# Spatial mixing spread between projections, and a first norm's vectors spread by other products

## The chip, the cores and the metric

The kernel runs on one core of a Trainium2 chip. The metric is the device time of one execution in microseconds. The kernel before takes 1092.2 us (median of three runs, 1090.23 to 1094.16). The profile comes from one further execution of 1090.98 us, whose traced span is 1089.2 us; some 1.8 us of it lie around the span.

Engines are named as in the profile: PE multiplies matrices, DVE and POOL work on vectors, ACT does activations and copies, SP and ACT issue the DMAs. Each engine works through its own instructions strictly in order and waits for others by semaphores.

## The reference

A layer norm, then two layers. One layer projects the normed stream (512 tokens, 1024 channels) by one wide matrix, mixes tokens in three ways, projects back and norms again:

```
h = layer_norm(x, ln_in_g, ln_in_b)
for l in range(2):                       # hybrid_layer
    na_q, na_k, na_v, na_z, gq_q, gq_k, gq_v, gq_z, sg_u, sg_v, sg_z, gates = split(h @ w_in + b_in)
    y_a = neighbourhood_attention(na_q, na_k, na_v, na_rpb)
    y_b = gqa_attention(rope(rms_norm(gq_q)), rope(rms_norm(gq_k)), gq_v)
    y_c = sg_u * (w_s @ layer_norm(sg_v) + b_s)      # per chunk of 128 tokens and group of 64 channels
    p_x = (y_x * silu(z_x)) @ w_br_x                 # x = a, b, c
    h = layer_norm(alpha * h + (sum of sigmoid(gate_x) * p_x) @ w_out + b_out)
```

The third mixer is the spatial mixing: a layer norm of `sg_v` over its 512 channels, then in each of four chunks of 128 tokens a product with a 128x128 matrix per channel group, then a sum with a bias. All of it is float32.

## The kernel before

Float32 accuracy on PE comes from splitting both factors into a rounded part (h, float32r) and the rest (l): each product is run three times, h by h, l by h and h by l (`mm3`, L195 to L198). Every weight chunk is loaded by SP as `raw_...`, its rounded part `whi_...` is copied by ACT (L143) and its rest `wlo_...` is subtracted by DVE (L144). A projection group such as `zb` (a gate), `nq`, `nk`, `su` or `sz` has 24 products of 128x128 by 128x512 into one bank of PSUM. PSUM banks come from two sets: `acc` with three buffers and `att` with five.

**The start** (`first_layer_start`, emitted and issued in written order). The rows `x` come in tiles of 128 tokens (`xin`). The first norm's scale and shift lie in DRAM as two rows of 1024. They are loaded to one partition (`lnrow`) and spread over all 128 partitions by four float32 products with a column of ones (`lnb`, L347), each recorded as two passes. DVE applies the norm to tile 0 straight from these four PSUM banks (L359 and L361, two operations for each half of 512 channels), ACT later copies them to `lnc_in` for the other tiles. The weights of the first queries come as four chunks `raw_gq_0` to `_3`; ACT rounds each ("high", L337), and the rest ("low", L340) is made on POOL for chunks 0 and 1 and on DVE for chunks 2 and 3. The power -0.5 of each norm's variance is a small POOL operation (`rs`, L226).

**The middle of a layer.** The work is written as a list of steps; Tile turns it into one order for each engine. First come ten projection chunks (`sv`, `nv`, `zb_0`, `zb_1`), with the rotation and transposes of the grouped-query heads between them (`between`). Then follow units of grouped-query attention: scores `gs`, their row maximum `nm` (DVE), the exponential with its sum (ACT, `gp`), reciprocal and scaling (DVE), transposes `gt` (PE) with copies `gpT` (ACT), and products with the values `gy`. Between units stand the steps of the list `fill`. Spatial mixing is in that list: for chunk c of the tokens n_c is the norm's first half (`svT` transposes on PE, BN_STATS and BN_AGGR on DVE, the power on POOL), and m_c is the rest: the normed chunk `vn` by two DVE operations (L233, which subtracts the mean and scales, and L235, which multiplies by `rs` and adds), eight products `mix` on PE (L536) and four sums `m` on DVE (L540).

Of the kernel before, what the change touches and what calls it, by code (L numbers as in the profile page):

```python
# [9 lines left out]
F32 = mybir.dt.float32  # L10
F32R = mybir.dt.float32r
AF = mybir.ActivationFunctionType
ALU = mybir.AluOpType
# [4 lines left out]
P = 128  # L18
D = 1024
KD = D // P  # L20
S = 512
NT = S // P
# [11 lines left out]
NCHUNK = 4  # L34
# [18 lines left out]
def tile_encoder(ctx: ExitStack, tc: tile.TileContext, a, out):  # L53
    nc = tc.nc
    scalar = nc.scalar
# [14 lines left out]
    act = nc.scalar.activation  # L70
    dve = nc.vector
    pool = nc.gpsimd
    pe = nc.tensor
# [12 lines left out]
    pw = cst.tile([P, 10], F32, name="pw")  # L86
    pool.memset(pw, -0.5)

    one = cst.tile([P, 1], F32, name="one")
    pool.memset(one, 1.0)  # L90
    bcol = cst.tile([P, DEPTH, NCOL], F32, name="bcol")
    hcol = cst.tile([P, DEPTH, NCOL], F32, name="hcol")
    bvg = cst.tile([P, DEPTH, NKV], F32, name="bvg")
# [20 lines left out]
    def psum(tag, name):  # L114
        return pp.tile([P, S], F32, tag=tag, name=name, bufs=3 if tag == "acc" else 5)

    def t2(name):
        return tp.tile([P, S], F32, tag="t2", name=name, bufs=4)
# [4 lines left out]
    def asf(r):  # L123
        return r.bitcast(F32)
# [25 lines left out]
    def step(fn, specs=(), frees=None, into=None):  # L150
        steps.append((fn, list(specs), len(specs) if frees is None else frees, into))
# [167 lines left out]
    def first_layer_start():  # L319
        raw = {}  # L320
        input_load(0)
        rows = rp.tile([P, 2, D], F32, tag="r8", name="lnrow")[0:1]
        scalar.dma_start(rows, a["ln_in_rows"])
        scalar.dma_start(ident, a["ident"])
        for n in ("q0", "q1", 1, "q2", "q3", 2, "k0", 3, "k1"):
            if isinstance(n, int):
                input_load(n)
            else:
                raw[n] = load(*(gqw_spec if n[0] == "q" else kvw_spec)(0, int(n[1])))
        w = {}  # L330

        def high(n):
            if n[0] == "q":
                w[n] = gqw_tile(f"gq0_{n[1]}")
            else:
                w[n] = [wp.tile([P, 4, 256], F32R, tag=t, name=f"{t}_gkv0_{n[1]}") for t in ("whi", "wlo")]
            act(w[n][0], raw[n], AF.Copy)  # L337

        def low(n, engine):
            engine.tensor_tensor(w[n][1], raw[n], asf(w[n][0]), op=ALU.subtract)  # L340

        gains = {}
        lnc = st["lnc"] = cst.tile([P, 2, D], F32, tag="cvec", name="lnc_in")
        for h in range(2):
            for j in range(2):
                ps = gains[j, h] = psum("acc" if h + j < 2 else "att", f"lnb_{h}_{j}")
                pe.matmul(ps, lhsT=one[0:1].broadcast_to([1, P]), rhs=rows[:, j, 512 * h:512 * h + 512],  # L347
                          start=True, stop=True)

        def stats(i):  # L350
            st["stats", i] = row_stats(st["xin", i], D, f"in{i}")

        def apply(i):
            xi, (mv, rs) = st["xin", i], st["stats", i]
            xt = []
            for h in range(2):
                cs = slice(512 * h, 512 * h + 512)
                g, b = [gains[j, h] if i == 0 else lnc[:, j, cs] for j in range(2)]
                dve.scalar_tensor_tensor(out=xi[:, cs], in0=xi[:, cs], scalar=mv[:, 0:1], in1=g,  # L359
                                         op0=ALU.subtract, op1=ALU.mult)  # L360
                dve.scalar_tensor_tensor(out=xi[:, cs], in0=xi[:, cs], scalar=rs, in1=b, op0=ALU.mult, op1=ALU.add)  # L361
                ps = psum("att", f"xt_in{i}_{h}")
                for j in range(4):
                    c = 512 * h + P * j
                    pe.transpose(ps[:, P * j:P * j + P], xi[:, c:c + P], ident)
                xt.append(ps)
            for h in range(2):
                split_x(xt[h], i, h)
            if i:
                scalar.dma_start(hbuf[0][i], xi)  # L370

        stats(0)
        high("q0")
        low("q0", pool)
        high("q1")
        low("q1", pool)
        apply(0)
        high("q2")
        low("q2", dve)
        stats(1)  # L380
        high("q3")
        low("q3", dve)
        for kc in range(4):
            st["gqw", kc] = w[f"q{kc}"]
        gq_queries(0, 0)
        for h in range(2):
            for j in range(2):
                act(lnc[:, j, 512 * h:512 * h + 512], gains[j, h], AF.Copy)
        scalar.dma_start(hbuf[0][0], st["xin", 0])
        apply(1)  # L390
        high("k0")
        low("k0", pool)
        stats(2)
        high("k1")
        low("k1", dve)
        st["kvw"] = w["k0"], w["k1"]
        gq_queries(0, 1)
        gq_keys_values(0, 0)
        apply(2)
        stats(3)  # L400
        gq_keys_values(0, 1)
        gq_queries(0, 2)
        apply(3)
        gq_keys_values(0, 2)
        gq_keys_values(0, 3)
        gq_queries(0, 3)

    def behind_start(l, f, i):
        if l or f is not gq_moments:
            return f(l, i)  # L410
        with tc.issue_after(st["last_xl"]):
            f(l, i)
# [105 lines left out]
    def sg_mix(l, c):  # L518
        def norm():
            if c == 0:  # L520
                st["m1"] = fp.tile([P, 4, S], F32, tag="f8", name=f"m1_{l}")
            ps = psum("acc", f"svT_{l}_{c}")
            for f in range(4):
                pe.transpose(ps[:, P * f:P * f + P], st["sv"][:, f, P * c:P * c + P], ident)
            st["vp", c] = ps, row_stats(ps, SGW, f"sg{l}_{c}")

        def mix():
            sgw, sgb, slg, slb = st["sg"]
            m1 = st["m1"]
            ps, stats = st["vp", c]  # L530
            vn = t2(f"vn_{l}_{c}")
            norm_apply(vn, ps, SGW, slg, slb, stats)
            pm = psum("acc", f"mix_{l}_{c}")
            for g in range(NSG):
                o = 64 * (g % 2)
                pe.matmul(pm[o:o + 64, P * (g // 2):P * (g // 2) + P], lhsT=vn[:, HD * g:HD * g + HD],  # L536
                          rhs=sgw[:, g, :], start=True, stop=True)
            for q in range(4):
                dst = m1[:, q, :].rearrange("p (b r c) -> p r b c", r=ROWS, c=8)[:, 2 * c:2 * c + 2]
                dve.tensor_tensor(dst, pm[:, P * q:P * q + P].rearrange("p (r b c) -> p r b c", r=2, c=8),  # L540
                                  sgb[:, q, :].rearrange("p (r b c) -> p r b c", r=2, c=8), op=ALU.add)
        return norm, mix
# [106 lines left out]
    def na_q(l, hp):  # L649
        c0 = C_NAQ + P * hp  # L650

        def fn(w):
            t = st["nqk", hp] = rp.tile([P, 2, 2, S], F32R, tag="r8", name=f"nqk_{l}_{hp}")
            ps = psum("acc", f"nq_{l}_{hp}")
            proj_fm(w, ps)
            for d0, s0, n in ((0, 448, 64), (64, 0, 448)):
                for e in range(2):
                    o, x = slice(64 * e, 64 * e + 64), slice(64 - 64 * e, 128 - 64 * e)
                    hi = t[o, 0, e, d0:d0 + n]
                    act(hi, ps[o, s0:s0 + n], AF.Identity, bias=bias(l, c0)[o])  # L660
                    dve.scalar_tensor_tensor(out=t[x, 0, e, d0:d0 + n], in0=ps[o, s0:s0 + n], scalar=bias(l, c0)[o],
                                             in1=asf(hi), op0=ALU.add, op1=ALU.subtract)
        return fn, [fm_spec(l, c0, f"nq{l}_{hp}")]
# [263 lines left out]
    for l in range(DEPTH):  # L927
        if l:
# [1 line left out]
        step(lambda l=l: layer_constants(l))  # L930
        chunks = [sg_value(l, f) for f in range(4)] + [na_value(l, f) for f in range(4)]
        chunks += [z_gate(l, "b", C_GZ, j) for j in range(2)]
        M, R, T = gq_moments, gq_rotate, gq_stack
        between = [[(M, 0)], [(M, 1)], [(R, 0)], [(T, 0), (M, 2)], [(R, 1)], [(T, 1), (M, 3)], [(R, 2)],
                   [(T, 2), (R, 3)], [(T, 3)], []]
        for c, fs in zip(chunks, between):
            for f, i in fs:
                step(lambda l=l, f=f, i=i: behind_start(l, f, i))
            step(*c)
        (n0, m0), (n1, m1), (n2, m2), (n3, m3) = [[(f,) for f in sg_mix(l, c)] for c in range(NCHUNK)]  # L940
        z = {j: z_gate(l, "b", C_GZ, j) for j in (2, 3)}
        u = [sg_out_u(l, j) for j in range(4)]
        g = [sg_out_z(l, j) for j in range(4)]
        fill = [n0, na_q(l, 0), n1, m0, n2, na_k(l, 0), m1, n3, m2, m3, u[0], u[1], g[0], u[2], z[2], g[1],
                u[3], z[3], g[2], g[3]]
        units = [(hp, t) for hp in range(NPAIR) for t in range(NT)]
        at = done = 0
        total = sum(len(f) - 1 for f in fill)
# [119 lines left out]
```

## Time and profile before

| | |
|---|---|
| median of runs | 1092.2 us |
| profiled execution, its span | 1090.98 us, 1089.2 us |
| PE busy | 1075.7 us, 99% of the span |
| DVE busy | 640.5 us, 59% |
| ACT busy | 470.6 us, 43% |
| POOL busy | 52.8 us, 5% |
| chain that ended last | PE 97%, DVE 2% |

Busy time of an engine is the time in which one of its instructions was in work. A PE product that follows another begins before the last one's record ends, so the pace of PE is read from start to start. DVE's 59% is a mean over stages: between 96 and 139 us, where layer 0's spatial mixing and grouped-query attention lie, it is busy 37.90 of 43 us. Layer 1 has the same stage about 533 us later.

### The profile page before, as it was taken

The page shows a single profiled execution, that of the slowest core. Times are in us where ns is not written, and L with a number is a line of the kernel's source. Part 1 is how long each engine was busy: PE and PEld are TensorE (multiplying, and loading weights), DVE is VectorE, ACT ScalarE, POOL GpSimd, SP SyncE. Part 2 cuts the span into 40 slices and gives each one's busy share as a digit, 9 for nine tenths or more (in the row PEclk, how much of TensorE's full clock was granted, in tenths as well). Part 3 has the DMA queues.
Part 4 walks back from the last instruction along what each step waited for, and adds up shares of the span by engine and source line. Part 5 has one row for each costly group of instructions (what it writes and reads, how often), then busy time and mean ns, then how long its engine had stood idle before and what let it go on. Part 6 is the DMA issues. An engine that isn't in the chain of part 4 may idle for free.

```text
span 1089.2 us, 14738 instructions
## 1 busy us (share of the span) xinstructions
PE 1075.7 (99%) x5744; PEld 887.8 (82%) x5744; DVE 640.5 (59%) x1205; ACT 470.6 (43%) x841; POOL 52.8 (5%) x54
## 2 busy tenths in 40 slices
PE   8999999999999999999999999999999999999997
PEld 5988788888888888888888887888888888888886
DVE  6775956665554543546876478566555555344465
ACT  4245735555655422334422365455645643223320
POOL 4420000000000000000021000000000000000001
PEclk9999999999999999999999999999999999999999
DMA  7522322213333433335652332222233334333421
GB/s 284 165 78 82 100 97 59 59 55 91 115 111 117 137 97 97 108 105 174 231 180 58 97 110 73 78 58 58 86 102 87 115 117 135 97 97 97 135 78 58
DMA packets 142808, 116.59 MB, mean 107 GB/s; under 512 B 4881, under 2 KB 130321, under 8 KB 142737
## 3 DMA queue, kind: packets, MB, share of 16 engines
q1 hardware_dynamic: 141872, 113.21, 33.5%
q10 hardware_dynamic: 866, 2.43, 0.6%
q8 instruction: 45, 0.74, 0.3%
q14 instruction: 25, 0.20, 0.1%
HBM read 109.34 MB, written 6.29 MB: 106 GB/s over the span
## 4 chain that ended last, share of the span: by engine, by line
PE 97%; DVE 2%; DMA 0%; issue 0%; ACT 0%; DVEq 0%
PE gq L306 4%; PE gy L735 3%; PE gb L196 3%; PE gc L198 3%; PE gc L197 3%; PE po L198 3%; PE po L197 3%; PE po L196 3%; PE gc L196 3%; PE ga L198 3%; PE ga L196 3%; PE gb L198 3%; PE gb L197 3%; PE ga L197 3%; PE gt L723 3%; PE gs L703 2%
## 5 line engine op out<-in xcount | busy, mean ns | idle before, releaser
L706 DVE TENSOR_REDUCE nm<-gs 128x1 f32<-128x512 f32 x64 | 42.3, 684 | 26.9 <-PE gs L704 26.8
L709 ACT ACTIVATE gp<-gs,nm 128x512 f32<-128x512 f32 x64 | 43.8, 688 | 21.4 <-DVE nm L706 19.8
L198 PE MATMUL gc<-xh,wlo_gc 128*128 128x512 f32 x128 | 51.1, 399 | 0.0
L725 ACT ACTIVATE gpT<-gt 128x512 f32<-128x512 f32 x64 | 36.7, 598 | 31.0 <-PE gt L723 30.8
L197 PE MATMUL gc<-xl,whi_gc 128*128 128x512 f32 x128 | 50.0, 391 | 0.0
L196 PE MATMUL gc<-xh,whi_gc 128*128 128x512 f32 x128 | 50.0, 391 | 0.0
L196 PE MATMUL gb<-xh,whi_gb 128*128 128x512 f32 x128 | 50.0, 391 | 0.0
L198 PE MATMUL gb<-xh,wlo_gb 128*128 128x512 f32 x128 | 49.8, 389 | 0.0
L197 PE MATMUL gb<-xl,whi_gb 128*128 128x512 f32 x128 | 49.8, 389 | 0.0
L196 PE MATMUL ga<-xh,whi_ga 128*128 128x512 f32 x128 | 49.8, 389 | 0.0
L198 PE MATMUL ga<-xh,wlo_ga 128*128 128x512 f32 x128 | 49.8, 389 | 0.0
L197 PE MATMUL ga<-xl,whi_ga 128*128 128x512 f32 x128 | 49.8, 389 | 0.0
L226 POOL TENSOR_TENSOR rs_po<-rs_po,pw 128x1 f32<-128x1 f32 x8 | 7.5, 939 | 814.4 <-DVE rs_po L225 814.4
L143 ACT ACTIVATE whi_gb<-raw_gb 128x1024 fp32r<-128x1024 f32 x16 | 17.0, 1060 | 60.4 <-PE pb L197 22.7
L779 ACT ACTIVATE nt<-nt,mx 128x256 f32<-128x256 f32 x64 | 30.1, 471 | 23.3 <-DVE mx L775 22.7
L144 DVE TENSOR_TENSOR wlo_ga<-raw_ga,whi_ga 128x1024 fp32r<-128x1024 f32 x16 | 19.6, 1222 | 33.5 <-ACT whi_ga L143 33.5
L735 PE MATMUL gy<-gpT,gv 128*64 128x128 f32 x512 | 38.8, 279 | 0.0
L723 PE MATMUL gt<-ident,gp 128*128 128x128 f32 x256 | 37.4, 276 | 0.7 <-ACT gpT L725 0.7
L735 PEld LDWEIGHTS gy<-gpT,gv 128*64 128x64 f32 x512 | 29.6, 136 | 10.2 <-issue 8.3
L144 DVE TENSOR_TENSOR wlo_gb<-raw_gb,whi_gb 128x1024 fp32r<-128x1024 f32 x16 | 19.6, 1222 | 30.1 <-ACT whi_gb L143 29.9
L723 PEld LDWEIGHTS gt<-ident,gp 128*128 128x128 f32 x256 | 29.7, 140 | 8.6 <-issue 2.7
L306 PE MATMUL gq<-w_gq,xh 128*128 128x512 f32 x128 | 34.0, 398 | 0.0
(282 smaller groups left out, 3099.0 us busy)
## 6 DMA issues: line engine op xcount, KB each, us to landing
raw_o<-in_w_out SPq DMA_DIRECT2D x24, 512.0 KB
raw_gc<-in_w_in SPq DMA_DIRECT2D x16, 512.0 KB
raw_gb<-in_w_in SPq DMA_DIRECT2D x16, 512.0 KB
raw_ga<-in_w_in SPq DMA_DIRECT2D x16, 512.0 KB
raw_gq<-in_w_in SPq DMA_DIRECT2D x8, 512.0 KB
raw_sv<-in_w_in SPq DMA_DIRECT2D x8, 512.0 KB
raw_nv<-in_w_in SPq DMA_DIRECT2D x8, 512.0 KB
raw_zb<-in_w_in SPq DMA_DIRECT2D x8, 512.0 KB
```

The costliest lines, as they stand in the source:

```text
L144: dve.tensor_tensor(wlo, raw, asf(whi), op=ALU.subtract)
L196: pe.matmul(ps, lhsT=lhi, rhs=rhi, start=first, stop=False)
L197: pe.matmul(ps, lhsT=lhi, rhs=rlo, start=False, stop=False)
L198: pe.matmul(ps, lhsT=llo, rhs=rhi, start=False, stop=last)
L306: pe.matmul(ps, lhsT=x[:, k, tk], rhs=w[p][k], start=n + k == 0, stop=n == 2 and k == KD - 1)
L703: pe.matmul(ps, lhsT=lhs, rhs=st["ks"][:, g, 0, :], start=True, stop=False)
L706: dve.tensor_reduce(out=nm, in_=ps, axis=AX.X, op=ALU.max, negate=True)
L709: act(pt, ps, AF.Exp, bias=nm, accum_out=sm)
L723: pe.transpose(ps[:, P * k:P * k + P], pt[:, P * k:P * k + P], ident)
L725: act(pT, ps, AF.Copy)
L735: pe.matmul(ps[64 * e:64 * e + 64, P * t:P * t + P], lhsT=st["gv"][:, k, HD * g:HD * g + HD], rhs=st["gp", hp, t, e][:, P * k:P * k + P], ...
L779: act(T[:, cs], T[:, cs], AF.Exp, bias=mx[:, i:i + 1], scale=SCALE, accum_out=sm[:, i:i + 1])
```

## The change

Two parts, in one diff.

At the start, the vectors are no longer spread from one partition. A DMA writes four rows of 512 (the halves of scale and shift) to 32 partitions each (`lnflat`, 128 partitions of 2 KB, 256 KB in all, against 8 KB before). ACT rounds it into `lnrow`, POOL subtracts the rest, and eight float32r products with weights of 1/32, each over 32 partitions, sum to the same four banks: four for the rounded part, four for the rest. The low part of chunk 3 moves from DVE to POOL and is emitted before tile 1's statistics.

In both layers the norms and sums of spatial mixing are emitted one at a time: `norm[0]` ahead of `zb_0`, `mix[0]` and `norm[1]` ahead of `zb_1`, and the others in `fill` in the new order. The third gate chunk `z[2]` moves from behind u[2] to before mix[3], so SP loads its weights earlier.

```
-    one = cst.tile([P, 1], F32, name="one")
-    pool.memset(one, 1.0)
...
-        rows = rp.tile([P, 2, D], F32, tag="r8", name="lnrow")[0:1]
-        scalar.dma_start(rows, a["ln_in_rows"])
+        rows = rp.tile([P, 3, S], F32R, tag="r8", name="lnrow")
+        one = rows[:, 2, 0:P]
+        pool.memset(asf(one), 1.0 / 32)
+        R = a["ln_in_rows"]
+        flat = t2("lnflat")
+        scalar.dma_start(flat, bass.AP(tensor=R.tensor, offset=R.offset, ap=[[S, 4], [0, 32], [1, S]]))
...
-        for h in range(2):
-            for j in range(2):
-                ps = gains[j, h] = psum("acc" if h + j < 2 else "att", f"lnb_{h}_{j}")
-                pe.matmul(ps, lhsT=one[0:1].broadcast_to([1, P]), rhs=rows[:, j, 512 * h:512 * h + 512],
-                          start=True, stop=True)
+        act(rows[:, 0], flat, AF.Copy)
+        pool.tensor_tensor(rows[:, 1], flat, asf(rows[:, 0]), op=ALU.subtract)
+        for p in range(2):
+            for h in range(2):
+                for j in range(2):
+                    q = 64 * h + 32 * j
+                    if p == 0:
+                        gains[j, h] = psum("acc" if h + j < 2 else "att", f"lnb_{h}_{j}")
+                    pe.matmul(gains[j, h], lhsT=one[q:q + 32], rhs=rows[q:q + 32, p],
+                              start=p == 0, stop=p == 1)
...
         low("q2", dve)
+        high("q3")
+        low("q3", pool)
         stats(1)
-        high("q3")
-        low("q3", dve)
...
+        norm, mix = [list(fs) for fs in zip(*[sg_mix(l, c) for c in range(NCHUNK)])]
...
-        between = [[(M, 0)], [(M, 1)], [(R, 0)], [(T, 0), (M, 2)], [(R, 1)], [(T, 1), (M, 3)], [(R, 2)],
-                   [(T, 2), (R, 3)], [(T, 3)], []]
+        between = [[M[0]], [M[1]], [R[0]], [T[0], M[2]], [R[1]], [T[1], M[3]], [R[2]], [T[2], R[3]],
+                   [T[3], norm[0]], [mix[0], norm[1]]]
...
-        fill = [n0, na_q(l, 0), n1, m0, n2, na_k(l, 0), m1, n3, m2, m3, u[0], u[1], g[0], u[2], z[2], g[1],
-                u[3], z[3], g[2], g[3]]
+        fill = [na_q(l, 0), (mix[1],), (norm[2],), na_k(l, 0), (mix[2],), (norm[3],), z[2], (mix[3],), u[0], u[1], g[0],
+                u[2], g[1], u[3], z[3], g[2], g[3]]
```

PE in layer 0, before, around the first `mix` (in the names the first number is the layer, the second the chunk, and the last only tells copies apart):

```order
L198 MATMUL nq_0_0_1016<-xh_92,wlo_nq0_0_939 128x512
L524 MATMUL svT_0_1_1049<-ident_78,sv_0_520 128x128 x4
L536 MATMUL mix_0_0_1064<-sgc_0_493,vn_0_0_1061 64x128 x8
L704 MATMUL gs_0_1_1_1153<-ks_0_502,qs_0_0_500 128x512
L723 MATMUL gt_0_0_0_0_1167<-ident_78,gp_0_0_0_979 128x128 x4
L723 MATMUL gt_0_0_0_1_1174<-ident_78,gp_0_1_0_987 128x128 x4
```

The same place after, from the last products of `zb_0` to the first of `zb_1`:

```order
L197 MATMUL zb_0_0_927<-xl_91,whi_zb0_0_851 128x512
L198 MATMUL zb_0_0_927<-xh_90,wlo_zb0_0_852 128x512
L712 MATMUL gs_0_0_0_1021<-ks_0_508,qs_0_0_506 128x512
L712 MATMUL gs_0_1_0_1029<-ks_0_508,qs_0_0_506 128x512
L712 MATMUL gs_0_0_1_1167<-ks_0_508,qs_0_0_506 128x512
L713 MATMUL gs_0_0_0_1021<-ks_0_508,qs_0_0_506 128x512
L713 MATMUL gs_0_1_0_1029<-ks_0_508,qs_0_0_506 128x512
L713 MATMUL gs_0_0_1_1167<-ks_0_508,qs_0_0_506 128x512
L712 MATMUL gs_0_1_1_1175<-ks_0_508,qs_0_0_506 128x512
L713 MATMUL gs_0_1_1_1175<-ks_0_508,qs_0_0_506 128x512
L545 MATMUL mix_0_0_960<-sgc_0_499,vn_0_0_957 64x128 x8
L533 MATMUL svT_0_1_973<-ident_78,sv_0_526 128x128 x4
```

The first `mix` stood behind `zb_0`, `zb_1` and `nq_0`; now it stands behind `zb_0` and eight scores products, and `svT` of chunk 1, `zb_1` and `nq_0` stand behind it.

DVE at the same place before: the operations from the splitting of `nq` to the second operation of `vn` of chunk 0, and the two behind it:

```order
L144 TENSOR_TENSOR wlo_nq0_0_939<-raw_nq0_0_797,whi_nq0_0_938 128x1024
L224 BN_AGGR mv_sg0_0_1003<-st_sg0_0_1002 128x2
L584 SCALAR_TENSOR_TENSOR zsb_0_0_935<-zthb_0_0_933,zsb_0_0_935 128x512
L496 TENSOR_TENSOR qs_0_1_501<-qT_0_3_880,qs_0_1_501 64x2x128
L225 TENSOR_SCALAR rs_sg0_0_1004<-mv_sg0_0_1003 128x1
L233 SCALAR_TENSOR_TENSOR vn_0_0_1061<-svT_0_0_997,mv_sg0_0_1003,sgc_0_493 128x512
L706 TENSOR_REDUCE nm_0_0_0_977<-gs_0_0_0_974 128x1
L706 TENSOR_REDUCE nm_0_1_0_985<-gs_0_1_0_982 128x1
L235 SCALAR_TENSOR_TENSOR vn_0_0_1061<-vn_0_0_1061,rs_sg0_0_1004,sgc_0_493 128x512
L144 TENSOR_TENSOR wlo_nk0_0_1010<-raw_nk0_0_849,whi_nk0_0_1009 128x1024
L706 TENSOR_REDUCE nm_0_0_1_1148<-gs_0_0_1_1145 128x1
```

DVE there after, from the last split of the keys `ks` on:

```order
L513 TENSOR_TENSOR ks_0_508<-kT_0_636,ks_0_508 64x512
L514 TENSOR_TENSOR ks_0_508<-kT_0_636,ks_0_508 64x512
L505 TENSOR_TENSOR qs_0_1_507<-qT_0_3_886,qs_0_1_507 64x2x128
L233 SCALAR_TENSOR_TENSOR vn_0_0_957<-svT_0_0_909,mv_sg0_0_915,sgc_0_499 128x512
L715 TENSOR_REDUCE nm_0_0_0_1024<-gs_0_0_0_1021 128x1
L144 TENSOR_TENSOR wlo_nq0_0_986<-raw_nq0_0_803,whi_nq0_0_985 128x1024
L715 TENSOR_REDUCE nm_0_1_0_1032<-gs_0_1_0_1029 128x1
L715 TENSOR_REDUCE nm_0_0_1_1170<-gs_0_0_1_1167 128x1
L715 TENSOR_REDUCE nm_0_1_1_1178<-gs_0_1_1_1175 128x1
L235 SCALAR_TENSOR_TENSOR vn_0_0_957<-vn_0_0_957,rs_sg0_0_916,sgc_0_499 128x512
L593 SCALAR_TENSOR_TENSOR zsb_0_0_954<-zthb_0_0_952,zsb_0_0_954 128x512
```

Between the last `ks` and the second operation of `vn` there stand one `qs`, the first operation of `vn`, four row maxima and the splitting of `nq`.

POOL at the start, before (`rs_in0` and `rs_in1` are the powers for tiles 0 and 1):

```order
L226 TENSOR_TENSOR rs_in0_136<-rs_in0_136,pw_79 128x1
L340 TENSOR_TENSOR w_gq0_0_142<-raw_gq0_0_107,w_gq0_0_142 128x1024
L340 TENSOR_TENSOR w_gq0_1_145<-raw_gq0_1_109,w_gq0_1_145 128x1024
L226 TENSOR_TENSOR rs_in1_171<-rs_in1_171,pw_79 128x1
L340 TENSOR_TENSOR wlo_gkv0_0_230<-raw_gkv0_0_119,whi_gkv0_0_229 128x1024
L226 TENSOR_TENSOR rs_in2_235<-rs_in2_235,pw_79 128x1
```

And after:

```order
L349 TENSOR_TENSOR lnrow_102<-lnflat_104,lnrow_102 128x512
L226 TENSOR_TENSOR rs_in0_142<-rs_in0_142,pw_79 128x1
L344 TENSOR_TENSOR w_gq0_0_148<-raw_gq0_0_107,w_gq0_0_148 128x1024
L344 TENSOR_TENSOR w_gq0_1_151<-raw_gq0_1_109,w_gq0_1_151 128x1024
L344 TENSOR_TENSOR w_gq0_3_175<-raw_gq0_3_115,w_gq0_3_175 128x1024
L226 TENSOR_TENSOR rs_in1_180<-rs_in1_180,pw_79 128x1
```

The subtraction for the vectors stands first, and chunk 3's low part stands ahead of the power for tile 1.

## Rows read from the trace of the kernel before

**Rows 1.** The page: busy time, share and instructions; the chain that ended last.

```profile
PE 1075.7 (99%) x5744; PEld 887.8 (82%) x5744; DVE 640.5 (59%) x1205; ACT 470.6 (43%) x841; POOL 52.8 (5%) x54
...
PE 97%; DVE 2%; DMA 0%; issue 0%; ACT 0%; DVEq 0%
```

**Rows 2.** By stretch: length; busy PE, PEld, DVE, ACT, POOL; granted clock; DMA share; GB/s.

```profile
3.50:10.60 7.10, 7.07 (x8) 2.48 (x8) 3.80 (x7) 2.11 (x2) 3.85 (x3) 1.00 1.04 396
...
96.00:139.00 43.00, 42.50 (x285) 34.10 (x284) 37.90 (x85) 29.17 (x59) 2.18 (x4) 1.00 0.29 84
640.00:672.00 32.00, 31.50 (x232) 25.02 (x231) 30.14 (x72) 20.24 (x42) 2.22 (x4) 1.00 0.31 89
```

**Rows 3.** Timeline of the start: start, duration, engine, line, work, idle before.

```profile
3.53 7.16 PE L347 MATMUL lnb<-lnrow,one 1*128 1x512 f32 x8 [3.53 <-DMA lnrow<-in_ln_in_rows]
...
4.70 1.29 DVE L223 BATCH_NORM_STATS2 st_in<-xin 128x6 f32<-128x512 f32 x2 [4.70 <-DMA xin<-in_x]
...
7.30 4.66 POOL L340 TENSOR_TENSOR w_gq<-raw_gq,w_gq 128x1024 fp32r<-128x1024 f32 x2 [0.18 <-ACT w_gq L337]
...
10.72 0.75 DVE L361 SCALAR_TENSOR_TENSOR xin<-xin,rs_in,lnb 128x512 f32<-128x512 f32 x1 [0.96 <-PE lnb L347]
...
11.77 0.60 ACT L249 ACTIVATE xh<-xt_in 128x512 fp32r<-128x512 f32 x1 [3.27 <-PE xt_in L365]
...
12.42 1.80 PE L306 MATMUL gq<-w_gq,xh 128*128 128x512 f32 x4
...
13.18 2.00 ACT L337 ACTIVATE w_gq<-raw_gq 128x1024 fp32r<-128x1024 f32 x2
...
14.06 1.09 PE L306 MATMUL gq<-w_gq,xl 128*128 128x512 f32 x4
...
17.04 1.23 DVE L340 TENSOR_TENSOR w_gq<-raw_gq,w_gq 128x1024 fp32r<-128x1024 f32 x1
17.19 1.48 POOL L226 TENSOR_TENSOR rs_in<-rs_in,pw 128x1 f32<-128x1 f32 x1 [5.23 <-DVE rs_in L225]
...
20.57 0.75 DVE L361 SCALAR_TENSOR_TENSOR xin<-xin,rs_in,lnc_in 128x512 f32<-128x512 f32 x1
```

**Rows 4.** Timeline of PE in layer 0, by single rows.

```profile
97.44 0.48 PE L196 MATMUL zb<-xh,whi_zb 128*128 128x512 f32 x1
...
103.02 0.39 PE L196 MATMUL zb<-xh,whi_zb 128*128 128x512 f32 x1
...
103.47 0.60 PE L524 MATMUL svT<-ident,sv 128*128 128x128 f32 x4
...
120.12 0.66 PE L723 MATMUL gt<-ident,gp 128*128 128x128 f32 x4 [0.31 <-ACT gpT L725]
...
121.39 0.50 PE L196 MATMUL nk<-xh,whi_nk 128*128 128x512 f32 x1 [0.18 <-DVE vn L233]
```

**Rows 5.** Timeline of DVE in layer 0, the same stage.

```profile
104.17 0.69 DVE L505 TENSOR_TENSOR ks<-kT,ks 64x512 fp32r<-64x512 f32 x1
104.89 0.42 DVE L496 TENSOR_TENSOR qs<-qT,qs 64x256 fp32r<-64x256 f32 x1
...
105.96 1.21 DVE L144 TENSOR_TENSOR wlo_nq<-raw_nq,whi_nq 128x1024 fp32r<-128x1024 f32 x1
...
108.51 0.75 DVE L233 SCALAR_TENSOR_TENSOR vn<-svT,mv_sg,sgc 128x512 f32<-128x512 f32 x1
109.57 1.29 DVE L706 TENSOR_REDUCE nm<-gs 128x1 f32<-128x512 f32 x2 [0.31 <-PE gs L704]
110.77 0.74 DVE L235 SCALAR_TENSOR_TENSOR vn<-vn,rs_sg,sgc 128x512 f32<-128x512 f32 x1
```

**Rows 6.** Busy time by stretch behind the last product (columns of group 2).

```profile
1085.00:1085.50 0.50, 0.00 (x0) 0.00 (x0) 0.50 (x2) 0.00 (x0) 0.00 (x0) 1.00 0.00 0
1085.50:1086.00 0.50, 0.00 (x0) 0.00 (x0) 0.50 (x1) 0.00 (x0) 0.00 (x0) 0.55 0.00 0
```

**Rows 7.** Timeline of PE at the end: its last product.

```profile
1081.73 0.28 PE L198 MATMUL po<-xh,mgl 128*128 128x256 f32 x1
```

More of the change, by code (lines that the diff above doesn't have):

```diff
@@ L932, in tile_encoder @@
         chunks += [z_gate(l, "b", C_GZ, j) for j in range(2)]
-        M, R, T = gq_moments, gq_rotate, gq_stack
-        between = [[(M, 0)], [(M, 1)], [(R, 0)], [(T, 0), (M, 2)], [(R, 1)], [(T, 1), (M, 3)], [(R, 2)],
-                   [(T, 2), (R, 3)], [(T, 3)], []]
+        norm, mix = [list(fs) for fs in zip(*[sg_mix(l, c) for c in range(NCHUNK)])]
+        M, R, T = [[lambda i=i, f=f, l=l: behind_start(l, f, i) for i in range(NT)]
+                   for f in (gq_moments, gq_rotate, gq_stack)]
+        between = [[M[0]], [M[1]], [R[0]], [T[0], M[2]], [R[1]], [T[1], M[3]], [R[2]], [T[2], R[3]],
+                   [T[3], norm[0]], [mix[0], norm[1]]]
         for c, fs in zip(chunks, between):
-            for f, i in fs:
-                step(lambda l=l, f=f, i=i: behind_start(l, f, i))
+            for f in fs:
+                step(f)
             step(*c)
-        (n0, m0), (n1, m1), (n2, m2), (n3, m3) = [[(f,) for f in sg_mix(l, c)] for c in range(NCHUNK)]
         z = {j: z_gate(l, "b", C_GZ, j) for j in (2, 3)}
@@ L1048 @@
     arrays["b_cols"] = np.ascontiguousarray(v["b_in"].reshape(DEPTH, NCOL, P).transpose(2, 0, 1))
-    arrays["ln_in_rows"] = np.ascontiguousarray(np.stack([v["ln_in_g"], v["ln_in_b"]])[None])
+    arrays["ln_in_rows"] = np.ascontiguousarray(np.stack([v["ln_in_g"], v["ln_in_b"]]).reshape(2, 2, S).transpose(1, 0, 2))
     bv = v["b_in"][:, C_GV:C_GV + P].reshape(DEPTH, NKV, HD).transpose(2, 0, 1)
```

## The prediction

> **What bounds the kernel now.** I read the page first: its chain of waits is 97% PE and 2% DVE, and PE is busy 99% of the span [rows 1]. So only three things can change the time: where PE stands idle, how fast its products run, and what it has to do. The second view is busy time by stretch: in the stage where spatial mixing lies, PE is idle for 0.50 us in layer 0 (42.50 of 43) and 0.50 us in layer 1 (31.50 of 32), while DVE is busy 88 to 94% of it [rows 2]. The timeline then says who PE waits for there: 0.31 us for a copy of ACT and 0.18 us for DVE's `vn` [rows 4]. Last I read the start, where PE is not idle by the record but works off long products: eight passes of `lnb` fill 7.16 us from 3.53, and DVE's last operation on tile 0 waits 0.96 us for them [rows 3]. PE's total work hardly changes, so the sum is made of waits.
>
> **The start.** Removed: the 7.16 us of `lnb`, which end at 10.69; DVE's last operation follows (10.72 to 11.47), ACT's `xh` at 11.77 and the first `gq` at 12.42 [rows 3]. Added is a chain. The 256 KB of `lnflat` land no earlier than 3.53 (when `lnrow` did) and, behind tile 0, which is there at 4.70, at about 5.4 (256 KB at the 396 GB/s of this stretch add 0.65) [rows 2, 3]. I take 4.7. ACT's copy of 128x512 costs 0.60, as `xh` does: 5.3. POOL's subtraction of 128x512 is half of one of the two that take 4.66: 1.17, so 6.5 [rows 3]. No row shows a float32r product over 32 partitions; its bounds are 0.27 and 0.45 us, the paces of the two `gq` rows at 14.06 and 12.42 [rows 3]. I take 0.45, that of a PE that has done little before. The four products of the rounded part lie beside POOL's subtraction; of the four of the rest, DVE needs the first at 7.0 and the others each 0.45 later, faster than it uses them (0.75 each). It would end at about 10.0 (7.0 and four times 0.75), against 11.47: 1.5 us earlier.
>
> What is late next: POOL's low part of chunk 3. It starts when ACT has rounded the chunk (15.18 before, some 13.8 as ACT's work moves forward with `xh`) and takes 2.33: 16.1. In the kernel before DVE ended this at 18.27, and POOL's power for tile 1, 1.48 us long beside it, at 18.67; tile 1 was ready at 21.32 [rows 3]. Behind POOL's low part the power stands 2.33 us longer in its queue than needed, yet ends by 16.7 to 17.6 (0.56, a third of the row's 1.48, for the first of these powers, up to the row's 1.48). Tile 1 is then ready at 18.8 to 19.7, a gain of 1.6 to 2.5. Against this, 256 KB more delay every later landing by 0.65, and POOL and DVE may slow each other. I take a gain of 1.5 us, that of the first link; the bounds are 2.5 gained and 0.5 lost. The cover that hides the rest is POOL, which is otherwise idle there.
>
> **The middle, per layer.** PE's instructions are the same ones in another order; what counts is that `mix` of chunk 0 now stands in PE's queue in front of `svT` of chunk 1, `zb_1` and `nq`. I put durations of before onto the new order, in the clock of before. Four transposes move ahead of `zb_0` (0.36, from 103.47 to the next product), which then starts at 97.8 instead of 97.44 and, with 5.58 us for its 24 products, ends at 103.4 [rows 4]. Eight scores products at 0.23 would end at 105.2; the last two need DVE's second split of `ks`, which ends at 104.86 and now has three operations of the first norm ahead of it in gaps that DVE had [rows 5]. So PE stands before `mix` at 105.4.
>
> DVE at that moment has `qs` just done (104.89 and 0.42: 105.31, so 105.4 with the shift). Before `mix` may start, its queue holds: first operation of `vn` 0.75, one row maximum 0.64, the splitting of `nq` 1.21, three row maxima 1.93, second operation of `vn` 0.74 [rows 5]. That is 5.27 us of work in a row, none of which PE needs except the two `vn`, and DVE is in order. From start to start DVE operations run some 0.06 closer than their durations add up to, which makes it 5.0; PE is idle for that time, since all behind `mix` stands in the same queue. Bounds: 4.5 if the `ks` splits come 0.5 later to PE as well, 5.5 if ACT's rounding of `nq` is late.
>
> The wait of before, 0.5 us per layer, goes: from the point where `mix` is done DVE has caught up. What is late next I walked the same way up to `su`: the four sums of chunk 0 end some 2.5 us before `nq` asks for their bank, the sums of chunk 1 1.5 us before `nk`, those of chunk 2 about 1.4 us before `zb_2`. All are estimates from the same durations; no second wait follows if they hold. SP's earlier load for `zb_2` is no cost: DMA is at 0.29 of its engines' time there [rows 2]. Net per layer: 5.0 − 0.5 = 4.5, for two layers 9.0. Layer 1 has the same order.
>
> **The clock.** Behind PE's last product (1081.73 and 0.28) the granted clock stays full to 1085.5 and is 0.55, then half, from there on [rows 6, 7]: behind an idle PE it drops to its lower level, 1.2 of 2.4 GHz. A wait at `mix` is idleness of the same kind. Products at the lower level are what the start shows: four took 1.80, the next four 1.09 [rows 3]. So a fall costs at least the 0.9 us by which four products are slower than at 0.23 each. No row shows a fall in mid-kernel. Bounds: nothing, or in each layer half of `zb_1`, 12 products at 0.22 more, 2.6 us, in all 5.3. I take 0.9 once, one fall in two waits.
>
> The Trainium skill, "TensorE: Matmul & The Clock Gate", Part 1 (The HAM clock gate), says that this clock knows only half and full and falls back to half after idleness. The tail's rows agree. By it alone both waits would end at half speed, and the sum would be that of rival A.
>
> **Sum.** −1.5 + 9.0 + 0.9 = +8.4 us. On the profiled execution's 1090.98 us that is 1099.4; on the median of the runs shown, which is 1.2 higher and against which a run of the new kernel stands, it is 1100.6. I take 1100.6.
>
> **Rivals.**
>
> A: the clock falls in both waits and stays low for half of `zb_1`. For it: the tail shows such a fall behind an idle PE. Against it: that is a single observation, and the other idle stretches of this trace are short. Time: 1100.6 − 0.9 + 5.3 = 1105.0.
>
> B: more waits behind the first, where my slack is smallest (`nk`, `zb_2`), since DVE has little room in this stage [rows 2]. A slip of 3 us in ACT's or DVE's queue would use the 1.5 up and cost 1.5 per layer: 1103.6.
>
> C, on the other side: DVE reaches the second `vn` operation before PE asks for it, so that the new order costs nothing and only the gains stay: −1.5 − 1.0 = 1089.7. It decides from the point where the wait at `mix` is under 1.25 us per layer (−1.5 + 2 × (1.25 − 0.5) = 0). For it: DVE loses time to ACT while `ks` is split, and could run ahead there. Against it: the two `ks` splits that PE's scores need stand in front of all 5.27 us, and nothing in the start's gain shifts the two queues against each other.
>
> D: the waits are real but half as long (1.25 to 2.5 each), and the start gives its upper bound: 1091 to 1094, no change.
>
> **Chances and range.** Forecast 0.55, A 0.25, B 0.08, C 0.06, D 0.06. The forecast's own range is 1098 to 1103 (start from 0.5 lost to 2.5 gained, waits 4.5 to 5.5, clock 0 to 1.8). A and B lie above, up to 1105; D and C below. The range 1096 to 1105 leaves out C, D and the upper half of A. Under 0.3% (3.3 us) a measurement of this kernel, whose three runs spread by 4 us, can't tell from no change: faster 0.06, same 0.06, slower 0.88.
>
> **What would show it.** Right: PE idle for 4.5 to 5.5 us right before the first `mix` of each layer, released by DVE's second `vn` operation; no PE wait over 0.5 us from there to `su`; the first `gq` at 10.5 to 11.5 and tile 1's transposes some 1.5 us earlier. The clock term shows in `zb_1`: 24 products in 5.6 us if the clock holds, more if it fell. Wrong: no wait at the first `mix`, or a wait released by something else; a start that is no shorter because the last low part on POOL comes later than 18.3.

## The result and the profile after

The changed kernel takes 1108.09 us (median of four runs, 1107.49 to 1108.41) against 1091.83 for the kernel before: 1.015 times, with a 95% interval of 1.0134 to 1.0165. That is slower by 16.3 us, where I had forecast 8.4 and a range up to 1105. The direction and the wait in the middle came as forecast; the start went the other way.

The page of the kernel after, busy time and chain, answers to [rows 1]:

```profile
PE 1072.4 (97%) x5744; PEld 888.4 (80%) x5744; DVE 641.3 (58%) x1204; ACT 470.3 (43%) x842; POOL 56.1 (5%) x56
...
PE 93%; DVE 2%; DMA 2%; ACT 1%; issue 1%; POOL 0%; SPq 0%; DVEq 0%; POOLq 0%; ACTq 0%
```

PE has 3.3 us less to do and yet the span is 16.5 us longer: nearly all of it is idleness, the rest slower products, shown below. What PE waited for (engine, line, what for, by whom; total, times, longest):

```profile
PE lnb L356 <- ACT lnrow L348: 11.6, 1, 11.6
PE mix L545 <- DVE vn L235: 9.2, 2, 4.6
PE xt_in L374 <- DVE xin L370: 3.8, 4, 1.7
PE gt L732 <- ACT gpT L734: 0.8, 2, 0.5
```

The first row is the start (in [rows 3] PE begins at 3.53), the second the two waits at the first `mix`, one per layer. The start, by its timeline (columns as in [rows 3]):

```profile
0.72 1.16 ACTq L327 DMA_DIRECT2D lnflat<-in_ln_in_rows  x1
...
10.85 0.63 ACT L348 ACTIVATE lnrow<-lnflat 128x512 fp32r<-128x512 f32 x1 [7.26 <-DMA lnflat<-in_ln_in_rows]
...
11.56 1.28 POOL L349 TENSOR_TENSOR lnrow<-lnflat,lnrow 128x512 fp32r<-128x512 f32 x1 [9.44 <-ACT lnrow L348]
11.62 0.80 PE L356 MATMUL lnb<-lnrow 32*128 32x512 f32 x4 [11.62 <-ACT lnrow L348]
...
12.89 0.80 PE L356 MATMUL lnb<-lnrow 32*128 32x512 f32 x4 [0.47 <-POOL lnrow L349]
...
17.68 2.00 PE L306 MATMUL gq<-w_gq,xh 128*128 128x512 f32 x4
...
25.65 0.75 DVE L370 SCALAR_TENSOR_TENSOR xin<-xin,rs_in,lnc_in 128x512 f32<-128x512 f32 x1
```

`lnflat` is issued at 0.72 and lands at 10.85. The products themselves are cheap: each group of four takes 0.80 us, the four beside each other, so 1.6 us in all against 7.16 for the old ones. Tile 1's last operation starts at 25.65 instead of 20.57 [rows 3], so the start costs 5.08 us. While the vectors are under way, the DMA engines stay busy but move less (columns as in [rows 2], which has 396 GB/s for the same stretch; the next row is the middle of layer 0):

```profile
3.50:10.60 7.10, 0.00 (x0) 0.00 (x0) 1.65 (x4) 0.09 (x1) 0.00 (x0) 1.00 1.05 291
...
96.00:144.00 48.00, 42.73 (x256) 34.50 (x254) 33.14 (x70) 26.47 (x52) 1.64 (x3) 0.96 0.25 72
```

PE around the first `mix` of layer 0, and in layer 1 the same `mix` and the fourth product of `zb_1`:

```profile
110.49 0.40 PE L713 MATMUL gs<-ks,qs 128*128 128x512 f32 x1
115.51 1.97 PE L545 MATMUL mix<-sgc,vn 128*64 128x128 f32 x16 [4.62 <-DVE vn L235]
117.41 1.12 PE L533 MATMUL svT<-ident,sv 128*128 128x128 f32 x4
118.18 0.61 PE L196 MATMUL zb<-xh,whi_zb 128*128 128x512 f32 x1
...
119.09 0.40 PE L196 MATMUL zb<-xh,whi_zb 128*128 128x512 f32 x1
...
129.73 1.09 PE L545 MATMUL mix<-sgc,vn 128*64 128x128 f32 x16
...
654.47 1.98 PE L545 MATMUL mix<-sgc,vn 128*64 128x128 f32 x16 [4.62 <-DVE vn L235]
...
658.23 0.39 PE L196 MATMUL zb<-xh,whi_zb 128*128 128x512 f32 x1
```

The wait is 4.62 us in both layers, and the first `mix` takes 1.97 where the second takes 1.09. The granted clock, the third number from the end of a row, says why (stretches of layer 0):

```profile
110.90:114.95 4.05, 0.00 (x0) 0.00 (x0) 4.05 (x7) 2.67 (x8) 0.00 (x0) 1.00 0.17 47
114.95:115.50 0.55, 0.00 (x0) 0.00 (x0) 0.55 (x2) 0.55 (x3) 0.00 (x0) 0.61 1.09 324
115.50:117.40 1.90, 1.89 (x16) 1.57 (x16) 1.84 (x8) 0.25 (x2) 0.00 (x0) 0.50 0.30 90
...
118.20:119.10 0.90, 0.90 (x6) 0.78 (x5) 0.89 (x5) 0.00 (x0) 0.00 (x0) 0.84 0.41 112
```

PE stands idle, the clock goes to half (0.50) shortly before `mix` comes, and it is full again after the first products of `zb_1`. In layer 1 it is 0.50 from 654.50 to 656.30 too. DVE in that wait does exactly what stood in its order (compare [rows 5]):

```profile
110.52 0.75 DVE L233 SCALAR_TENSOR_TENSOR vn<-svT,mv_sg,sgc 128x512 f32<-128x512 f32 x1
111.19 0.68 DVE L715 TENSOR_REDUCE nm<-gs 128x1 f32<-128x512 f32 x1
111.79 1.21 DVE L144 TENSOR_TENSOR wlo_nq<-raw_nq,whi_nq 128x1024 fp32r<-128x1024 f32 x1
112.92 1.88 DVE L715 TENSOR_REDUCE nm<-gs 128x1 f32<-128x512 f32 x3
114.72 0.74 DVE L235 SCALAR_TENSOR_TENSOR vn<-vn,rs_sg,sgc 128x512 f32<-128x512 f32 x1
```

PE's last product moves from 1081.73 [rows 7] to 1098.22, by 16.49 us: 5.08 from the start and 11.41 from the two layers.

### The profile page after: what moved, and what is told of

The parts are those of the page before. It is cut to its first block, busy times and chain, and to the rows that moved or that the text cites. A ratio compares the mean times of both kernels' runs of the same rounds, so it can differ in the third digit from the quotient of the medians.

```text
span 1105.7 us, 14742 instructions
## 1 busy us (share of the span) xinstructions
PE 1072.4 (97%) x5744; PEld 888.4 (80%) x5744; DVE 641.3 (58%) x1204; ACT 470.3 (43%) x842; POOL 56.1 (5%) x56
## 2 busy tenths in 40 slices
DMA packets 142938, 116.84 MB, mean 106 GB/s; under 512 B 4884, under 2 KB 130324, under 8 KB 142868
## 4 chain that ended last, share of the span: by engine, by line
PE 93%; DVE 2%; DMA 2%; ACT 1%; issue 1%; POOL 0%; SPq 0%; DVEq 0%; POOLq 0%; ACTq 0%
PE gq L306 3%; PE gy L744 3%; PE gb L196 3%; PE gc L197 3%; PE po L197 3%; PE gc L196 3%; PE po L198 3%; PE po L196 3%; PE gc L198 3%; PE ga L196 3%; PE gb L198 3%; PE gb L197 3%; PE ga L198 3%; PE ga L197 3%; PE gt L732 2%; PE su L196 1%
```

## The experiments

Times are medians; ratios are against the kernel before, measured again beside each group of runs (1091.0 to 1091.1 us).

**The two parts apart.** `start_alone` keeps the list of steps of the kernel before, `middle_alone` its start.

> The start of the changed kernel with the middle of the kernel before. Theory (the two parts add up; the start costs what the first gq of tile 1 moved, 26.93 against 21.85): 5.1 us over before, the vectors landing near 10.8 us. Rival (part of the loss comes from the two parts together, such as the later input loads): 2 us or less, or over 8.

> The middle of the changed kernel with the start of the kernel before. Theory (a wait of 4.6 us at the first mix of each layer, a fall of the clock worth 1.7 us in each, less 0.5 us of old waits): 11 us over before, both first mix records near 2 us instead of 1.1. Rival (the clock falls in only one layer when the phase of the kernel is another, or the waits came from the start's delay): 8 us or less.

Measured: 1097.55 us, 1.0061 (1.0046 to 1.0076), and 1102.72 us, 1.0112 (1.0094 to 1.0129). The middle's wait at `mix` is 4.62 in both layers again, so it owes nothing to the start. The two excesses add up to 1.0173, the changed kernel has 1.0150; the difference lies within the three intervals.

The start alone costs 6.5 us, more than the 5.1 expected. In its trace tile 1's first `gq` is 4.85 late (26.70 against 21.85), but PE's last product 6.13 (1087.86 against 1081.73): behind the new start the old middle loses another 1.3 us. Some 0.5 of it is waits at `gt` (1.2 us in two, 0.7 before); the rest is not accounted for.

**Why the vectors land late.** My first theory was that 32 packets read the same 2 KB. The first test changed too much:

```
-        scalar.dma_start(flat, bass.AP(tensor=R.tensor, offset=R.offset, ap=[[S, 4], [0, 32], [1, S]]))
+        scalar.dma_start(flat, a["w_in"][1][0:P, 0:S])          # distinct_rows
```

> As start_alone, but the 256 KB come from 128 different rows of 2 KB (of a weight matrix, so the first norm gets sums of weights for its scale and shift) and not from four rows read 32 times each. Theory same address (the packets are slow because 32 of them read one row of 2 KB): the tile lands by 6 us, the stretch from 5 to 10 us moves near 390 GB/s again, the time is at most 1 us over before. Rival second queue (256 KB on the second queue get a small share of busy DMA engines, whatever they read): it lands near 10 us as before and the time stays 5 us over before.

Measured: 1091.9 us, 1.0013 (1.0004 to 1.0023); the tile is there at 5.16. That looked like the theory come true. But the new source also has another shape, 128 rows in one step instead of four blocks. A second pair separates the two (the outermost size, the second number of the first pair, is 32 in the first line and 4 in the second):

```
+            ap=[[0, 32], [S, 4], [1, S]]                        # same_rows_32first
+            ap=[[33 * W.ap[0][0], 4], [W.ap[0][0], 32], [1, S]] # distinct_4first, W = a["w_in"][1]
```

> As start_alone, but the DMA of the vectors walks its source with 32 repeats outermost and the four rows inside them: still 128 packets of 2 KB from four rows, each read 32 times, now with an outermost size of 32 instead of 4 (the first norm gets the mean of the four rows in every bank). Theory same address: nothing changes, the tile lands near 10 us, 5 us or more over before. Rival few engines (a DMA whose outermost size is 4 runs on 4 of the 16 DMA engines, and there it alternates with the loads of the other queue; the Trainium skill, DMA: Bandwidth & Descriptors, section on why a DMA increments its semaphore by 16, gives such a rule): the tile lands by 5.5 us and the time is within 1.5 us of before.

> As distinct_rows, 128 different rows of 2 KB, but walked as four blocks of 32 rows that do not join up, so the outermost size is 4 (the first norm gets sums of weights). Theory same address: as distinct_rows, the tile lands by 5.5 us, within 1.5 us of before. Rival few engines: the tile lands near 10 us and the time is 5 us or more over before, although no row is read twice.

Measured: 1091.25 us, 1.0005 (0.9995 to 1.0014), and 1098.64 us, 1.0070 (1.0055 to 1.0085). ACT's copy of the tile, whose start is the landing, in `same_rows_32first`:

```profile
4.96 0.63 ACT L348 ACTIVATE lnrow<-lnflat 128x512 fp32r<-128x512 f32 x1 [1.65 <-DMA lnflat<-in_ln_in_rows]
```

and in `distinct_4first`:

```profile
11.64 0.63 ACT L349 ACTIVATE lnrow<-lnflat 128x512 fp32r<-128x512 f32 x1 [8.02 <-DMA lnflat<-in_w_in]
```

| landing, us | outermost size 4 | outermost size 32 or 128 |
|---|---|---|
| four rows, 32 times each | 10.61 (start_alone) | 4.96 (same_rows_32first) |
| 128 different rows | 11.64 (distinct_4first) | 5.16 (distinct_rows) |

The address theory falls: which rows are read moves the landing by about 1.0 us at most, the outermost size of the source by 5.7 to 6.5. So does the other rival on record, that a second queue gets a small share whatever it reads: all four loads go by that queue. The Trainium skill, "DMA: Bandwidth & Descriptors", section "Why a DMA increments its semaphore by 16 and not by 1", says that a DMA is split over the largest number of engines, up to 16, that divides the outermost sizes of both its sides; for 4 and 128 that is 4 of 16 engines. The table agrees.

The rows of the ACT queue on the profiles' pages (packets, MB, share) bear it out, in order `start_alone`, `same_rows_32first` and, from the next group, `four_dmas`:

```profile
q10 hardware_dynamic: 996, 2.69, 0.7%
q10 hardware_dynamic: 1008, 2.69, 0.6%
q10 hardware_dynamic: 1056, 2.69, 0.6%
```

For the same 128 rows the second has 12 packets more than the first, all under 512 bytes (4896 such packets on its page, 4884 on the other); `distinct_rows` has 1008 and `distinct_4first` 996. Twelve is 16 less 4, one small packet for each engine that takes part. That reading is an inference: no view names the engine of a packet.

**Other ways to load.** `four_rows` loads only the four rows, 8 KB, into a tile that DVE has zeroed; `four_dmas` uses four DMAs of 32 partitions.

```
+        dve.memset(flat, 0.0)                                   # four_rows, weights 1 instead of 1/32
+        scalar.dma_start(<partitions 0, 32, 64, 96 of flat>, <four rows of R>)
...
+        for q in range(4):                                      # four_dmas
+            scalar.dma_start(flat[32 * q:32 * q + 32], bass.AP(tensor=R.tensor, offset=R.offset + S * q, ap=[[0, 32], [1, S]]))
```

> As start_alone, but only the four rows themselves are loaded (8 KB to partitions 0, 32, 64 and 96 of a tile that DVE has set to zero) and the weights are 1. The copy, the subtraction and the eight products are unchanged. Both theories: the rows land by 5 us, since 8 KB have few packets; if all the loss of the start is the landing, the time is 1 to 2 us under before (the first gq near 11). If the products or POOL's low part of chunk 3 cost as well, it is not under before.

> As start_alone, but four DMAs of 32 partitions, each reading one row 32 times, so that every outermost size is 32. Theory same address: lands near 10 us, 5 us over before. Rival few engines: every DMA runs on 16 engines, the last is issued about 1.5 us later than the one of start_alone and lands by 6.5 us; time within 2 us of before, without any copy of the rows in DRAM.

Measured: 1092.62 us, 1.0017 (1.0008 to 1.0026), the rows there at 6.00; and 1097.12 us, 1.0057 (1.0042 to 1.0072). The first missed its 5 us and its gain; its DMA waits for the zeroing and is issued at 1.42 instead of 0.72. The second contradicts what the rival that the pair above has borne out expected of it; its ACT rows:

```profile
0.72 2.15 ACTq L328 DMA_DIRECT2D lnflat<-in_ln_in_rows  x4
4.95 0.36 ACTq L329 DMA_DIRECT2D ident<-in_ident  x1
9.67 1.28 ACT L349 ACT_TABLE_LOAD   x1 [9.67 <-DMA lnflat<-in_ln_in_rows]
```

The last of the four had landed by 9.67, and the queue's next DMA was not issued before 4.95. Outermost sizes of 32 were thus not enough here, though by the count above (1056, 48 more than 1008) each of the four used 16 engines. The pieces ran one behind the other: the ACT queue moved 48 packets before 4.0 us (32 rows and 16 small ones), 48 from 4.0 to 6.0, and the rest later. Why a piece of 64 KB takes that long there stays open.

**What the start is worth with the landing mended.** `rep_rows_q3dve` lays the rows out 32 times in DRAM and gives chunk 3's low part back to DVE.

```
-    ... .reshape(2, 2, S).transpose(1, 0, 2))
+    ... .reshape(2, 2, S).transpose(1, 0, 2).reshape(4, 1, S).repeat(32, axis=1).reshape(P, S))
```

> The new start with the vectors' rows laid out 32 times in DRAM, so that 128 different rows of 2 KB are read, and chunk 3's low part back on DVE behind tile 1's statistics; middle of the kernel before. Theory (with different rows the tile lands by 5.2 us; POOL's low part of 2.5 us then set the end of the start in distinct_rows): tile 1's first gq starts at about 20.6 to 21.2 and the time is 0 to 1 us under before. Rival (DVE is the one that is late in either case): gq starts no earlier than 21.2.

Measured: 1092.1 us, 1.0010 (0.9999 to 1.0022); tile 1's first `gq` at 21.91, 21.85 before. No gain, the rival's side. With the low part on POOL it is at 21.43 with the same rows (`both_mended`, below) and at 21.23 in `distinct_rows`. But the five traces that have the old start (`before`, `middle_alone` and the three `mid_` runs below) show this row from 20.82 to 21.92, so none of these differences is a gain that the traces can tell. The timeline of `distinct_rows`, PE, DVE and POOL:

```profile
11.99 2.06 PE L306 MATMUL gq<-w_gq,xh 128*128 128x512 f32 x4
...
13.84 1.91 PE L306 MATMUL gq<-w_gq,xl 128*128 128x512 f32 x4
```

```profile
8.02 0.75 DVE L368 SCALAR_TENSOR_TENSOR xin<-xin,mv_in,lnb 128x512 f32<-128x512 f32 x1 [1.35 <-PE lnb L356]
...
10.42 0.75 DVE L370 SCALAR_TENSOR_TENSOR xin<-xin,rs_in,lnb 128x512 f32<-128x512 f32 x1
```

```profile
14.94 2.50 POOL L344 TENSOR_TENSOR w_gq<-raw_gq,w_gq 128x1024 fp32r<-128x1024 f32 x1 [2.45 <-ACT w_gq L341]
17.39 1.01 POOL L226 TENSOR_TENSOR rs_in<-rs_in,pw 128x1 f32<-128x1 f32 x1
```

The first `gq` is only 0.4 us earlier than in [rows 3], and the power for tile 1 stands behind POOL's 2.50 us until 17.39. The second four products take 1.91, there 1.09; but with the old start they take 1.09 to 1.77, so a slow pace there is not the new start's alone. By PE's last product `distinct_rows` is 0.52 late (1082.25 against 1081.73): as in `start_alone` the old middle loses time behind the new start, 0.6 of it in waits at `gt` (1.3 us in two, 0.7 before).

**The middle: what makes the wait, and what the clock costs.** `mid_filler` puts 16 products, whose result is overwritten, in front of the first `mix` (and holds `svT` of chunk 1 behind it); `mid_vn_first` orders the four row maxima behind `vn`; `mid_mix0_late` moves one step. All three have the start of before.

```
+            if c == 0:                                          # mid_filler, in mix()
+                for n in range(16):
+                    pe.matmul(pm, lhsT=q1[:, 3 * P:4 * P], rhs=q1, start=True, stop=True)
...
+        if h < 2 and t < 2:                                     # mid_vn_first, in gqa_scores()
+            tc.add_manual_dep(top.ins, st["vn2"].name, <order only>)
...
-                   [T[3], norm[0]], [mix[0], norm[1]]]
+                   [T[3], norm[0]], [norm[1]]]                  # mid_mix0_late
...
-        fill = [na_q(l, 0), (mix[1],), ...
+        fill = [(mix[0],), na_q(l, 0), (mix[1],), ...
```

> As middle_alone (11 us over before), but PE runs 16 products of 128x128 by 128x512, whose result is overwritten, in front of the first mix of each layer, about 3.7 of the 4.6 us of the wait. Theory (1.7 us per layer is a fall of the clock because PE stands idle): the granted clock stays full, both mix records return to 1.1 us, the rest of the wait is about 0.9 us, and the time falls by 3 to 3.5 us against middle_alone. Rival (the wait alone makes the loss, and mix is slow there for another reason, such as a cold weight load): no change against middle_alone.

> As middle_alone, but the four row maxima of the first unit are ordered behind the second operation of vn on DVE; vn's first operation, the splitting of nq and vn's second remain in front of mix. Theory (the wait is the DVE work in front of vn's second operation): it falls by the four maxima, 2.5 us, to about 2.1; the clock no longer falls; the time is 4 us or more under middle_alone, if the maxima, now later, do not make a new wait. Rival (the wait is set by the power on POOL or by ACT's rounding of nq): 4 us or more of wait remain.

> As middle_alone, but the first mix is taken out of its place ahead of zb_1 and put first in the list behind the projections; PE then has it behind zb_1 and the first unit. Theory (only the place of this one mix loses time): no wait over 0.7 us in the middle, clock full, time within 1.5 us of before. Rival (emitting norms and sums one at a time loads DVE worse throughout): waits move to nq, nk or zb_2, 3 us or more over before.

`mid_filler`: 1097.43 us, 1.0054 (1.0037 to 1.0071), 5.3 us under `middle_alone`, more than the 3 to 3.5 forecast; the span of the profiled execution is 3.6 us shorter. Its PE rows:

```profile
105.40 3.80 PE L539 MATMUL mix<-qs 128*128 128x512 f32 x16
110.18 1.09 PE L543 MATMUL mix<-sgc,vn 128*64 128x128 f32 x16 [0.98 <-DVE vn L235]
111.21 0.66 PE L524 MATMUL svT<-ident,sv 128*128 128x128 f32 x4
...
112.41 0.40 PE L196 MATMUL zb<-xh,whi_zb 128*128 128x512 f32 x1
```

`mix` starts no earlier against the stage, but it runs at full pace, with a granted clock of 1.00: work that serves nothing makes the kernel faster, since PE does not stand idle. From `mix` to the fourth product of `zb_1` it takes 2.23 us; in the changed kernel 3.58 in layer 0 (115.51 to 119.09) and 3.76 in layer 1 (654.47 to 658.23), in `middle_alone` 3.79 and 4.11. So a fall of the clock costs 1.35 to 1.9 us. The rest of the 5.3 is not accounted for; the profiled execution of `middle_alone` is its fastest (1100.98 us at a mean granted clock of 0.994), the three others take 1102.47 to 1103.73 at 0.992, so there the falls may cost more.

`mid_vn_first`: 1095.57 us, 1.0038 (1.0025 to 1.0050), 7.2 us under `middle_alone`. The wait falls by 2.39 us in both layers, about the four maxima (0.68 and 1.88):

```profile
107.89 1.09 PE L538 MATMUL mix<-sgc,vn 128*64 128x128 f32 x16 [2.23 <-DVE vn L235]
...
642.81 1.98 PE L538 MATMUL mix<-sgc,vn 128*64 128x128 f32 x16 [2.23 <-DVE vn L235]
```

That the clock no longer falls came true in layer 0 alone. In layer 1, behind a wait of the same 2.23 us, `mix` runs at half pace and the granted clock is 0.50 from 642.85 to 644.70. The eight executions take 1094.25 to 1097.38 us at mean granted clocks of 0.998 to 0.994, so the number of falls seems to change from one to the next.

`mid_mix0_late`: 1090.7 us, 0.9993 (0.9984 to 1.0002). What PE waits for in it, behind the start:

```profile
PE gt L723 <- ACT gpT L725: 0.6, 2, 0.3
PE zb L196 <- ACT zsb L583: 0.4, 2, 0.2
```

One step moved behind `zb_1`, and the whole loss of the middle is gone.

**Both mended.** The replicated rows with POOL's low part, and the late first `mix`:

> The changed kernel with its two losses taken out: the rows laid out 32 times in DRAM (128 different rows read, chunk 3's low part on POOL), and the first mix put behind the projections. Theory (losses add up and nothing else in the change costs): no PE wait over 0.7 us in the middle, tile 1's first gq near 21.2, time 0.5 to 1.5 us under before, 16 to 17 us under the changed kernel. Rival (a part of the loss comes from something in both, or the start's gain is given back in the middle as in distinct_rows): within 0.5 us of before or over it.

Measured: 1091.04 us, 0.9996 (0.9987 to 1.0005), 17 us under the changed kernel and no faster than before: the rival's side. Its tile 1 starts `gq` at 21.43, 0.4 early, which is less than the traces can tell. No version of the change beat the kernel before by more than the measurement can tell.

## Why the prediction was wrong

The step that failed is the landing: "the 256 KB of `lnflat` land no earlier than 3.53 ... and ... at about 5.4. I take 4.7". They landed at 10.85. I had priced the transfer by its bytes at the 396 GB/s of the stretch, whatever its shape. The runs show that bytes were not the matter: the same 256 KB land at 4.96 or 10.61 by the outermost size of the source alone, and the time falls by 6.3 us with the landing (1097.55 to 1091.25). The term −1.5 came out as +5.1, which is 6.6 of the 7.9 us that were missing.

Even with the landing mended, the gain of 1.5 was too large: at most 0.6 was there, within the spread of the traces, and no time was gained. I had let DVE's four operations run from 7.0 to 10.0; in `distinct_rows` they run from 8.02 to 11.17, against an end of 11.47 before. The landing (5.16 for 4.7), POOL's subtraction (ended at 7.14 for 6.5) and the products behind it (0.80 for the group, where I had 0.45 for the first alone) were each a little later. That POOL's low part with the power behind it would be late next was right, though it came later than forecast: the power ran from 17.39 to 18.40, where I had it end by 16.7 to 17.6.

The wait at the first `mix` was right in place, releaser and size: 4.62 in both layers, forecast 5.0 with bounds of 4.5 to 5.5. `mid_vn_first` shows its cause, the DVE queue ahead of `vn`'s second operation, by shortening it, and `mid_mix0_late` shows that only the place of this one `mix` makes PE wait for it.

The clock was mis-sized. I took 0.9 us once; it fell in both layers and cost 1.35 and 1.53, 2.9 in all. That was the first half of rival A's condition at about half its price (5.3): the clock did not stay low for half of `zb_1` but was full again after its first products. The rule that the prediction drew from the Trainium skill, "TensorE: Matmul & The Clock Gate", Part 1 (The HAM clock gate), that idleness brings the clock back to half, fits the rows of both waits. As put there it does not say which wait is long enough: in `mid_vn_first` one wait of 2.23 us brought a fall and an equal one did not. That the first products of the start ran at the lower level was read from their pace alone; the granted clock shows 1.00 there.

The old waits of 0.5 per layer did not all go: 0.52 and 0.23 us for ACT's copy remain at another `gt`. By these sizes layer 0 costs 4.62 + 1.35 − 0.5 + 0.52 and layer 1 4.62 + 1.53 − 0.5 + 0.23, 11.9 together; the trace has 11.41, and the 0.5 between them is not accounted for.

Rivals B, C and D did not come: no wait over 0.52 follows up to `su`, the slack that I walked held, and the waits were neither gone nor halved. C's state exists, though, one step away: it is `mid_mix0_late`, with the price that C gave the middle, nothing lost, but without a gain that can be measured.

One sum of the prediction was wrong beside the point: the ends that it names for the forecast's own range (start 2.5 gained to 0.5 lost, waits 4.5 to 5.5, clock 0 to 1.8) add up to 1097.7 and 1104.5, not to 1098 and 1103.

## What to carry to other kernels

When work is moved forward on PE, read the other engine's queue up to the instruction that PE will then wait for; its durations in the old trace, added up in the new order, gave this wait to within 0.4 us. Price a new DMA by its shape as well as its bytes, put the large dimension outermost, and keep it in one DMA: four pieces were no better here. An idle stretch on PE costs more than its length when the clock falls in it, and a wait of 2.23 us was long enough for that in one layer of two. Before a shift of a few tenths of a microsecond counts as a gain, look how far the same row moves between traces of unchanged code.

## What was not expected of the hardware

A DMA of 256 KB whose source has an outermost size of 4 needed 10 us beside the loads of the other queue, and the whole stretch moved 291 GB/s instead of 396 (389 in `same_rows_32first`) while the DMA engines were counted busy all the time (share 1.05). Products over 32 partitions in four row groups ran beside each other: four of 512 columns in 0.80 us, where in the same start four `gq` products over 128 partitions took 2.00 (17.68).
